# One layer of a hybrid decoder on one core: values transposed straight from their projection, and S5's output products tied to the next step

## The chip, the cores and the metric

The kernel runs on one core of one Trainium2 chip. The metric is the device time of one execution in microseconds, the median over several. PE is TensorE, DVE is VectorE, ACT is ScalarE, POOL is GpSimd, and SP is SyncE, which issues loads. Each engine works through its own queue in order and waits on semaphores that other engines and DMAs raise.

## The reference

One layer, 1024 tokens of width 1024. A normalised input `h` is projected once; two token mixers read the projection, S5 (a diagonal complex state space model) and DSA (attention over the 256 keys that an indexer scores highest); both are gated, merged and projected out.

```python
def hybrid_layer(x, c, ...):
    shift, scale, gate = jnp.split(jax.nn.silu(c) @ w_mod + b_mod, 3, axis=-1)
    h = rms_norm(x, norm_g) * (1 + scale) + shift
    xa, za, q, k, v, zb, qi, ki, wi, ga, gb = jnp.split(h @ w_in, IN_SPLITS, axis=-1)
    ya = jax.nn.gelu(s5_mixer(xa, a_re, a_im, b_re, b_im, c_re, c_im, d_skip, log_dt))
    g = ya @ w_glu + b_glu
    ya = ((g[..., :512] * jax.nn.sigmoid(g[..., 512:])) * jax.nn.silu(za)) @ w_a_o
    yb = dsa_mixer(q, k, v, qi, ki, wi)          # 8 query heads, one key and value head of 64
    yb = (yb * jax.nn.silu(zb)) @ w_b_o
    merged = jax.nn.sigmoid(ga) * ya + jax.nn.sigmoid(gb) * yb
    return x + gate * (merged @ w_out)
# s5_mixer: h_t = A h_(t-1) + B u_t per group of 16 channels (64 complex states), y_t = Re(C h_t) + D u_t
# dsa_mixer: score = sum over index heads of w * relu(qi . ki); keep the top 256 causal keys; softmax(q . k) v
```

## The kernel before, in words

All large products keep fp32 accuracy by splitting each operand in a high and a low half and multiplying three times, high by high, high by low and low by high (`three`, lines 137 to 139). A weight tile arrives as `*_w` from SP's queue, ACT casts the high half `*_wh`, DVE subtracts for the low half `*_wl` (`split`, lines 77 and 78). `project` makes one 128-row slice of the projection in two pieces of 512 tokens, 24 of these dense matmuls each, 48 a slice.

The input is transposed and normalised first, then xa, qi and ki are projected and the indexer's scores made, up to about 183 us. From there three things run beside each other until about 450 us:

- The **dense projections** on PE: q1 to q3, kv (keys in rows 0 to 63, values in rows 64 to 127), ga0 to ga7, gb0, gb1, zb0 to zb3. Their results leave through ACT (`gates`, lines 706 to 714) into a staging buffer of 128x1024 fp32, of which the pool `stage` has three, and are spilled to memory.
- The **S5 loop** (lines 584 to 683): eight steps q of four groups each. POOL prepares `mt` and `en` (lines 601 to 611). PE transposes `mt` (L614), and makes the kernel `k` (L621). ACT copies k, POOL adds the skip term (L630), and eight small DMAs from ACT's queue lay it out as the block matrix `mk` (L633). PE makes the states' input `s` (L637), ACT copies it out as `sp` (L643), DVE rotates, scans and rotates back (lines 655 to 672) and leaves the states `hs` (four subtractions and additions, the last of L672). PE then makes y from `mk` and the input (L676) and from `en` and `hs` (L678), four pairs into one bank, and ACT applies gelu and stores `yd`. `hs` has one buffer, `en` and `mk` have two.
- The **search** for the 256th score on DVE: twelve bisection steps of counts over the scores (`count`, L770), then the exact choice (lines 815 to 821). It ends in a flag `rows_ok` by which all engines branch; a slower path is taken only when the flag says so.

The order of instructions on each engine is made by the framework's scheduler, which follows data dependences, `order(later, earlier)` (an ordering without a wait) and `pace`, which ties dense matmuls behind given leads. Pools of buffers give further waits.

The values' way before: ACT copies rows 64 to 127 of kv into the staged tile `vraw` (`with_v`, L700), which is stored to memory as `vd` (L704). After the gate products (L737) a staged tile `vt` is loaded from `vd` (L751), once a staging buffer is free; PE transposes it in eight pieces into `v_ps` (L754), ACT and DVE split it into the halves of `v_s` (L77, L78). Then PE adds up the flag (L829), DVE casts it to `rows_ok` (L831), loads it to a register and branches (L833), and attention starts with the logits `l` (L894) and DVE's `S` (L897), with the dense matmuls of gb2 beside them.

Of the kernel before, what the change touches and what calls it, by code (L numbers as in the profile page):

```python
# [9 lines left out]
F32 = mybir.dt.float32  # L10
F32R = mybir.dt.float32r
BF = mybir.dt.bfloat16
I32 = mybir.dt.int32
AF = mybir.ActivationFunctionType
# [6 lines left out]
L = 1024  # L21
NT = L // 128
# [12 lines left out]
def tile_hybrid(ctx, tc, x, c, norm_g, w_mod, b_mod, w_in, a_re, a_im, b_re, b_im,  # L35
                c_re, c_im, d_skip, log_dt, w_glu, b_glu, w_a_o, w_b_o, w_out,
                final_g, out):
    nc = tc.nc
# [15 lines left out]
    spill = ctx.enter_context(tc.tile_pool(name="spill", bufs=1, space=DRAM))  # L54

    def bank(name):
        return ps1.tile([128, 512], F32, name=name, tag="b1")
# [10 lines left out]
    ident = const.tile([128, 128], F32, name="ident")  # L68
# [4 lines left out]
    def staged(name, dtype=F32, shape=(128, L)):  # L73
        return stage.tile(list(shape), dtype, name=name, tag="sg")

    def split(src, hi, lo, hi_eng=None, lo_eng=None):
        (hi_eng or nc.scalar.copy)(hi, src)  # L77
        (lo_eng or nc.vector).tensor_sub(lo, src, f32(hi))  # L78

    def order(later, earlier):  # L80

        tc.add_manual_dep(later.ins, earlier.ins.name, mybir.DependencyInfo(
            mybir.DependencyClass.NoSync, mybir.DependencyReason.DATA), reason="order")
# [78 lines left out]
    yds = []  # L162
    qd = spill.tile([8, 128, L], F32, name="qd")
    kd = spill.tile([2, 128, L], F32, name="kd")
    vd = spill.tile([64, L], F32, name="vd")
    zad = spill.tile([4, 128, L], F32, name="zad")
    zbd = spill.tile([4, 128, L], F32, name="zbd")
    gad = spill.tile([ND, 128, L], F32, name="gad")
# [3 lines left out]
    p2 = s5.enter_context(tc.tile_pool(name="p2a", bufs=1))  # L172
# [168 lines left out]
    with ExitStack() as st:  # L341
# [117 lines left out]
        ps = bank("wi_ps")  # L459
# [121 lines left out]
    mks = [p2.tile([128, 4, T, 16], F32, name=f"mk{e}") for e in range(2)]  # L581
    for mk in mks:
        nc.gpsimd.memset(mk, 0.0)
    for m in range(4):
        u_sb = p2.tile([128, 8, 128], F32, name=f"u{m}", tag="u", bufs=2)
        nc.scalar.dma_start(u_sb, uds[m].rearrange("g p s c -> (p s) g c"))
        yd = spill.tile([T, 16, 8, 128], F32, name=f"yd{m}")
        for half in range(2):
# [45 lines left out]

            ps = bank(f"s{q}_ps")
            for g in range(4):
                nc.tensor.matmul(ps[:, 128 * g:128 * g + 128], mi[:, g], us[:, g],  # L637
                                 start=True, stop=True)
            sp = p2.tile([128, 2, 2, 128], F32, name=f"sp{q}", tag="sp", bufs=2)
            pv = ps.rearrange("p (j e c) -> p e j c", j=2, e=2)  # L640
            for e in range(2):
# [27 lines left out]
            for e in range(2):  # L669
                a = slice(64 * e, 64 * e + 64)  # L670
                nc.vector.tensor_sub(hs[0:64, e:4:2, 1:], ra[a, 0, :, 0:127], rb[a, 1, :, 0:127])
                nc.vector.tensor_add(hs[64:128, e:4:2, 1:], ra[a, 1, :, 0:127], rb[a, 0, :, 0:127])  # L672
            ps = bank(f"y{q}_ps")
            for g in range(4):
                o = ps[:, 128 * g:128 * g + 128]
                nc.tensor.matmul(o, mk[:, g].rearrange("p t q -> p (t q)"), us[:, g],  # L676
                                 start=True, stop=False)
                nc.tensor.matmul(o, en[:, g, 1:9].rearrange("p t q -> p (t q)"), hs[:, g],  # L678
                                 start=False, stop=True)
            yg = p2.tile([128, 4, 128], F32, name=f"yg{q}", tag="yg", bufs=1)  # L680
            nc.scalar.activation(yg.rearrange("p g c -> p (g c)"), ps, AF.Gelu_apprx_tanh)
            nc.scalar.dma_start(yd[:, :, 4 * half:4 * half + 4].rearrange("t p g c -> (t p) g c"), yg)
        yds.append(yd)


    pace([], 0)
# [14 lines left out]
            yield ps, sl  # L701

    stack_k(with_v(project(w_in, K, 128, h_hi, h_lo, ND, "kv")), kd[0], kd[1], "k")
    nc.scalar.dma_start(vd, t[64:128])  # L704

    def gates(c0, ms, dst, silu, name):

# [38 lines left out]
    nc.sync.dma_start(f32(att_k), kd.rearrange("e p n -> p e n"))  # L746
    att_q = staged("qt0", F32R, (128, 8, 128))
    nc.sync.dma_start(f32(att_q), qd[:, :, 0:128].rearrange("h p n -> p h n"))
    att_v = kpool.tile([128, NT, 128], F32R, name="v_s")
    vt = staged("vt")  # L750
    nc.sync.dma_start(vt[0:64], vd)  # L751
    ps = bank("v_ps")
    for j in range(NT):
        nc.tensor.transpose(ps[:, 64 * j:64 * j + 64], vt[0:64, 128 * j:128 * j + 128], ident[:64, :64])  # L754
    split(ps.rearrange("p (j d) -> p j d", j=NT), att_v[:, :, 0:64], att_v[:, :, 64:128])


    for i in range(2):
# [351 lines left out]
```

## Time and profile before

| what | value |
|---|---|
| median of 3 runs | 911.64 us (910.56 to 913.61) |
| profiled execution, own time | 913.2 us |
| its span, first to last instruction | 911.4 us |
| mean granted clock of TensorE | 0.975 |
| instructions | 12005 |
| busy: DVE, ACT, POOL | 655.6 us (72%), 406.5 us (45%), 138.2 us (15%) |

The profile is of one execution. It lists busy time by engine, waits by line with the event that ended them, and the clock that TensorE was granted, as a share of 2.4 GHz. A wait at the head of an engine's queue holds up everything behind it on that engine. Idle time of an engine matters only where another engine, or the end, waits for it.

### The profile page before, as it was taken

To read this page: it belongs to the slowest core of one execution; us is meant where nothing else is said; L and a number is where in the kernel's file an instruction comes from. 1 tells how busy PE (TensorE), PEld (TensorE's weight loads), DVE (VectorE), ACT (ScalarE), POOL (GpSimd) and SP (SyncE) were. 2 spreads that over 40 slices of the span, in tenths; PEclk is the share of its full clock that TensorE was granted. 3 is DMA by queue.
4 is the path that set the end of the run, shared out by engine and by line. 5 is a ranking of instruction groups with operands and counts; after the bars stand their busy time and mean duration, and the time that the engine had idled before them with its cause. 6 is when DMAs were issued, how large, how long until landed. Compare 5 with 4: busy or idle time off the path is not lost.

```text
span 911.4 us, 12005 instructions
## 1 busy us (share of the span) xinstructions
PE 853.0 (94%) x4105; PEld 703.9 (77%) x4105; DVE 655.6 (72%) x1381; ACT 406.5 (45%) x803; POOL 138.2 (15%) x244
## 2 busy tenths in 40 slices
PE   4999999989889998999769999999999999999996
PEld 4887788877668877888558888887888888777885
DVE  5665898498989894687226677668987786956753
ACT  7553576354355542332225564457555443432311
POOL 0000100079446943000000000000000000221000
PEclk9799999999999998999969999999999999999999
DMA  9925611463443332573423323135314323644331
GB/s 328 315 65 131 147 49 47 74 181 89 121 117 119 110 111 65 183 263 92 116 70 97 92 83 112 47 105 151 103 47 129 92 81 93 198 150 149 139 131 54
DMA packets 124388, 110.38 MB, mean 121 GB/s; under 512 B 20954, under 2 KB 108066, under 8 KB 124324
## 3 DMA queue, kind: packets, MB, share of 16 engines
q1 hardware_dynamic: 96386, 77.46, 28.3%
q10 hardware_dynamic: 27938, 32.13, 12.0%
q8 instruction: 32, 0.52, 0.2%
q14 instruction: 32, 0.26, 0.1%
HBM read 76.67 MB, written 26.48 MB: 113 GB/s over the span
## 4 chain that ended last, share of the span: by engine, by line
PE 52%; DVE 13%; issue 4%; DMA 4%; ACT 2%; ACTq 2%; POOL 0%; DVEq 0%; SPq 0%
PE l L894 4%; DVE cj L770 3%; PE gb_ps L137 3%; PE gb_ps L138 3%; PE gb_ps L139 3%; PE pt L919 3%; PE o_ps L139 3%; PE o_ps L138 3%; PE o_ps L137 3%; PE pv L939 2%; PE pv L938 2%; PE ao_ps L139 2%; PE ao_ps L137 2%; PE ao_ps L138 2%; PE zb_ps L138 2%
## 5 line engine op out<-in xcount | busy, mean ns | idle before, releaser
L78 POOL TENSOR_TENSOR wo_l<-wo,wo_h 128x1024 fp32r<-128x1024 f32 x5 | 12.2, 2447 | 459.0 <-ACT wo_h L77 429.8
L770 DVE TENSOR_SCALAR_CACHE_REDUCE cj<-score,mid 128x1024 bf16<-128x1024 f32 (+2 forms) x72 | 67.6, 939 | 14.2 <-ACT mid L793 8.8
L897 DVE CUSTOM_DVE_ANT_0 S<-l,bias 128x384 f32<-128x384 f32 (+5 forms) x96 | 52.6, 553 | 26.5 <-PE l L894 23.4
L908 ACT ACTIVATE S<-S,stt 128x128 f32<-128x128 f32 (+7 forms) x64 | 49.1, 770 | 40.1 <-DVE stt L905 39.9
L77 ACT CAST ph<-pt 128x512 fp32r<-128x512 f32 x72 | 41.3, 584 | 43.4 <-PE pt L919 38.4
L78 DVE TENSOR_TENSOR pl<-pt,ph 128x512 fp32r<-128x512 f32 x72 | 48.8, 686 | 9.1 <-ACT ph L77 8.7
L894 PE MATMUL l<-k_s,qt 128*128 128x384 f32 (+5 forms) x192 | 50.2, 349 | 4.9 <-issue 4.9
L138 PE MATMUL gb_ps<-h_lo,gb_wh 128*128 128x512 f32 x128 | 51.4, 402 | 0.0
L137 PE MATMUL gb_ps<-h_hi,gb_wh 128*128 128x512 f32 x128 | 51.4, 401 | 0.0
L138 PE MATMUL o_ps<-wo_l,m_hi 128*128 128x512 f32 (+1 forms) x136 | 51.3, 378 | 0.0
L139 PE MATMUL o_ps<-wo_h,m_lo 128*128 128x512 f32 (+1 forms) x136 | 51.0, 377 | 0.1
L139 PE MATMUL gb_ps<-h_hi,gb_wl 128*128 128x512 f32 x128 | 51.1, 399 | 0.0
L139 PE MATMUL ga_ps<-h_hi,ga_wl 128*128 128x512 f32 x128 | 50.9, 397 | 0.0
L137 PE MATMUL ga_ps<-h_hi,ga_wh 128*128 128x512 f32 x128 | 50.7, 396 | 0.0
L138 PE MATMUL ga_ps<-h_lo,ga_wh 128*128 128x512 f32 x128 | 50.3, 393 | 0.0
L475 ACT ACTIVATE r<-s 128x512 f32<-128x512 f32 (+3 forms) x80 | 39.7, 525 | 23.2 <-PE s L471 15.4
L137 PE MATMUL o_ps<-wo_h,m_hi 128*128 128x512 f32 (+1 forms) x136 | 49.4, 377 | 0.2 <-ACT wo_h L77 0.2
L480 DVE SCALAR_TENSOR_TENSOR score<-r,wi_t,score 128x512 f32<-128x512 f32 (+3 forms) x70 | 42.1, 652 | 7.5 <-ACT r L475 6.6
L919 PE MATMUL pt<-ident,S 128*128 128x128 f32 x288 | 46.1, 272 | 0.0
L919 PEld LDWEIGHTS pt<-ident,S 128*128 128x128 f32 x288 | 36.5, 140 | 10.4
L471 PE MATMUL s<-ki_s,qi_s 128*128 128x384 f32 (+3 forms) x160 | 42.1, 355 | 1.8 <-DVE wi_t L464 1.3
L894 PEld LDWEIGHTS l<-k_s,qt 128*128 128x128 f32 x192 | 34.4, 191 | 10.4 <-issue 5.0
(402 smaller groups left out, 2400.7 us busy)
## 6 DMA issues: line engine op xcount, KB each, us to landing
wm<-in_w_mod_dram SPq DMA_DIRECT2D x16, 512.0 KB, 6.5
x_sb<-in_x_dram SPq DMA_DIRECT2D x8, 512.0 KB, 5.4
ga_w<-in_w_in_dram SPq DMA_DIRECT2D x8, 512.0 KB, 4.0
gad<-gas ACTq DMA_DIRECT2D x8, 512.0 KB, 2.6
gb_w<-in_w_in_dram SPq DMA_DIRECT2D x8, 512.0 KB, 4.4
wg<-in_w_mod_dram SPq DMA_DIRECT2D x8, 512.0 KB, 4.8
gbd<-gbs ACTq DMA_DIRECT2D x8, 512.0 KB, 3.1
qt<-qd SPq DMA_DIRECT2D x8, 512.0 KB, 4.0
```

The lines of the kernel that those rows point to most:

```text
L77: (hi_eng or nc.scalar.copy)(hi, src)
L78: (lo_eng or nc.vector).tensor_sub(lo, src, f32(hi))
L137: paced(nc.tensor.matmul(ps, wh, rh, start=first, stop=False))
L138: paced(nc.tensor.matmul(ps, wh, rl, start=False, stop=False))
L139: mm = nc.tensor.matmul(ps, wl, rh, start=False, stop=last)
L471: mm = nc.tensor.matmul(ps[:, :n], qs[:, h, 128 * i:128 * i + 128], ks[:, e, o:o + n], start=e == 0, stop=e == 1)
L480: nc.vector.scalar_tensor_tensor(dst, r[:, :n], wi_t[:, i, h:h + 1], dst, op0=OP.mult, op1=OP.add)
L770: nc.vector.tensor_scalar(j, src, at, None, op0=op, op1=OP.add, accum_out=dst)
L894: mm = nc.tensor.matmul(ps[:, :n], qt[:, 4 * e2 + 2 * j + g], ks[:, e, o:o + n], start=e == 0, stop=e == 1)
L897: nc.vector.tensor_tensor_reduce(out=S[:, o:o + n], in0=ps[:, :n], in1=bias[i][:, o:o + n], scale=1.0, scalar=NEG, op0=OP.add, op1=OP.max, ...
L908: nc.scalar.activation(S2[j], S2[j], AF.Exp, scale=0.125, bias=nm[:, j:j + 1], accum_out=sm[:, j:j + 1])
L919: mm = nc.tensor.transpose(ps[:, 128 * j:128 * j + 128], Ss[i, g, j][:, 128 * kb:128 * kb + 128], ident)
```

## The change

`vd`, `vt` and their two DMAs are gone: the transposes read rows 64 to 127 of the staged `vraw` tile, with the matching corner of the identity, and stand in the program right behind the keys' spill. The y products, their gelu and their store move to a function `outputs`, which is called in the following step behind the s products; its first matmul is ordered behind the last s product. The last call stands behind the loop.

```diff
@@ -162,7 +162,6 @@
     yds = []
     qd = spill.tile([8, 128, L], F32, name="qd")
     kd = spill.tile([2, 128, L], F32, name="kd")
-    vd = spill.tile([64, L], F32, name="vd")
     zad = spill.tile([4, 128, L], F32, name="zad")
     zbd = spill.tile([4, 128, L], F32, name="zbd")
     gad = spill.tile([ND, 128, L], F32, name="gad")
@@ -581,6 +580,23 @@
     mks = [p2.tile([128, 4, T, 16], F32, name=f"mk{e}") for e in range(2)]
     for mk in mks:
         nc.gpsimd.memset(mk, 0.0)
+    ready = []
+
+    def outputs(q, half, mk, us, en, hs, yd, behind_):
+
+        ps = bank(f"y{q}_ps")
+        for g in range(4):
+            o = ps[:, 128 * g:128 * g + 128]
+            mm = nc.tensor.matmul(o, mk[:, g].rearrange("p t q -> p (t q)"), us[:, g],
+                                  start=True, stop=False)
+            if g == 0:
+                order(mm, behind_)
+            nc.tensor.matmul(o, en[:, g, 1:9].rearrange("p t q -> p (t q)"), hs[:, g],
+                             start=False, stop=True)
+        yg = p2.tile([128, 4, 128], F32, name=f"yg{q}", tag="yg", bufs=1)
+        nc.scalar.activation(yg.rearrange("p g c -> p (g c)"), ps, AF.Gelu_apprx_tanh)
+        nc.scalar.dma_start(yd[:, :, 4 * half:4 * half + 4].rearrange("t p g c -> (t p) g c"), yg)
+
     for m in range(4):
         u_sb = p2.tile([128, 8, 128], F32, name=f"u{m}", tag="u", bufs=2)
         nc.scalar.dma_start(u_sb, uds[m].rearrange("g p s c -> (p s) g c"))
@@ -634,8 +650,10 @@
 
             ps = bank(f"s{q}_ps")
             for g in range(4):
-                nc.tensor.matmul(ps[:, 128 * g:128 * g + 128], mi[:, g], us[:, g],
-                                 start=True, stop=True)
+                last_s = nc.tensor.matmul(ps[:, 128 * g:128 * g + 128], mi[:, g], us[:, g],
+                                          start=True, stop=True)
+            if ready:
+                outputs(*ready.pop(), last_s)
             sp = p2.tile([128, 2, 2, 128], F32, name=f"sp{q}", tag="sp", bufs=2)
             pv = ps.rearrange("p (j e c) -> p e j c", j=2, e=2)
             for e in range(2):
@@ -670,17 +688,9 @@
                 a = slice(64 * e, 64 * e + 64)
                 nc.vector.tensor_sub(hs[0:64, e:4:2, 1:], ra[a, 0, :, 0:127], rb[a, 1, :, 0:127])
                 nc.vector.tensor_add(hs[64:128, e:4:2, 1:], ra[a, 1, :, 0:127], rb[a, 0, :, 0:127])
-            ps = bank(f"y{q}_ps")
-            for g in range(4):
-                o = ps[:, 128 * g:128 * g + 128]
-                nc.tensor.matmul(o, mk[:, g].rearrange("p t q -> p (t q)"), us[:, g],
-                                 start=True, stop=False)
-                nc.tensor.matmul(o, en[:, g, 1:9].rearrange("p t q -> p (t q)"), hs[:, g],
-                                 start=False, stop=True)
-            yg = p2.tile([128, 4, 128], F32, name=f"yg{q}", tag="yg", bufs=1)
-            nc.scalar.activation(yg.rearrange("p g c -> p (g c)"), ps, AF.Gelu_apprx_tanh)
-            nc.scalar.dma_start(yd[:, :, 4 * half:4 * half + 4].rearrange("t p g c -> (t p) g c"), yg)
+            ready.append((q, half, mk, us, en, hs, yd))
         yds.append(yd)
+    outputs(*ready.pop(), last_s)
 
 
     pace([], 0)
@@ -701,7 +711,12 @@
             yield ps, sl
 
     stack_k(with_v(project(w_in, K, 128, h_hi, h_lo, ND, "kv")), kd[0], kd[1], "k")
-    nc.scalar.dma_start(vd, t[64:128])
+
+    att_v = kpool.tile([128, NT, 128], F32R, name="v_s")
+    ps = bank("v_ps")
+    for j in range(NT):
+        nc.tensor.transpose(ps[:, 64 * j:64 * j + 64], t[64:128, 128 * j:128 * j + 128], ident[64:128, 64:128])
+    split(ps.rearrange("p (j d) -> p j d", j=NT), att_v[:, :, 0:64], att_v[:, :, 64:128])
 
     def gates(c0, ms, dst, silu, name):
 
@@ -746,13 +761,6 @@
     nc.sync.dma_start(f32(att_k), kd.rearrange("e p n -> p e n"))
     att_q = staged("qt0", F32R, (128, 8, 128))
     nc.sync.dma_start(f32(att_q), qd[:, :, 0:128].rearrange("h p n -> p h n"))
-    att_v = kpool.tile([128, NT, 128], F32R, name="v_s")
-    vt = staged("vt")
-    nc.sync.dma_start(vt[0:64], vd)
-    ps = bank("v_ps")
-    for j in range(NT):
-        nc.tensor.transpose(ps[:, 64 * j:64 * j + 64], vt[0:64, 128 * j:128 * j + 128], ident[:64, :64])
-    split(ps.rearrange("p (j d) -> p j d", j=NT), att_v[:, :, 0:64], att_v[:, :, 64:128])
 
 
     for i in range(2):
```

On PE the order around y5 moves so (a letter and number name a tile and the step q; hs5 are step 5's states, ga4 and ga5 dense projections). Before, 22 dense matmuls lie between the last y4 product and the first y5 product that reads hs5; these rows follow them:

```order
L139 MATMUL ga5_ps_3350<-h_hi3_249,ga5_wl_3321 128x512
L678 MATMUL y5_ps_2501<-hs5_2495,en5_2438 128x128
L676 MATMUL y5_ps_2501<-u2_2290,mk1_1901 128x128
L678 MATMUL y5_ps_2501<-hs5_2495,en5_2438 128x128
L676 MATMUL y5_ps_2501<-u2_2290,mk1_1901 128x128
L678 MATMUL y5_ps_2501<-hs5_2495,en5_2438 128x128
L676 MATMUL y5_ps_2501<-u2_2290,mk1_1901 128x128
L678 MATMUL y5_ps_2501<-hs5_2495,en5_2438 128x128
L621 MATMUL k6_ps_2534<-en6_2521,bx_1809 16x128 x4
L637 MATMUL s6_ps_2552<-u3_2513,mi6_2532 128x128 x4
L137 MATMUL ga5_ps_3350<-h_hi4_250,ga5_wh_3320 128x512
```

Now 32 dense matmuls lie between the last y4 product and these rows:

```order
L139 MATMUL ga5_ps_3360<-h_hi6_251,ga5_wl_3331 128x512
L637 MATMUL k6_ps_2521<-en6_2508,bx_1808 16x128 x4
L653 MATMUL s6_ps_2539<-u3_2500,mi6_2519 128x128 x4
L590 MATMUL y5_ps_2544<-u2_2277,mk1_1900 128x128
L594 MATMUL y5_ps_2544<-hs5_2494,en5_2425 128x128
L590 MATMUL y5_ps_2544<-u2_2277,mk1_1900 128x128
L594 MATMUL y5_ps_2544<-hs5_2494,en5_2425 128x128
L590 MATMUL y5_ps_2544<-u2_2277,mk1_1900 128x128
L594 MATMUL y5_ps_2544<-hs5_2494,en5_2425 128x128
L590 MATMUL y5_ps_2544<-u2_2277,mk1_1900 128x128
L594 MATMUL y5_ps_2544<-hs5_2494,en5_2425 128x128
L630 MATMUL mt7_ps_2594<-ident_75,mt7_2583 128x128 x4
```

y5's products moved from ahead of k6 and s6 to behind them, all eight together, and come 10 dense matmuls later. Counted in dense matmuls from the start of the program, the last products of y0 to y7 stand behind 655, 687, 756, 815, 926, 948, 998 and 1085 before, and behind 690, 722, 756, 821, 925, 957, 1011 and 1052 now. The first transposes of mt1 move from behind 588 to straight behind s0, at 531. POOL's instructions mu2, mt2, eu2 and mt3, which stood at the end of the rotation tables' products (lines 571 to 576) and behind it, stand among them now.

On PE the passage into attention, before:

```order
L139 MATMUL zb3_ps_3864<-h_hi7_253,zb3_wl_3834 128x512
L737 MATMUL gate0_3894<-gsum_3497,ones_80 1x512
L737 MATMUL gate1_3897<-gsum_3497,ones_80 1x512
L754 MATMUL v_ps_3915<-ident_75,vt_3913 128x64 x8
L829 MATMUL flag_ps_4358<-ones_80,sound_4354 1x1
L833 UNCONDITIONAL_BRANCH
L894 MATMUL l0_0_0_0_0_4958<-k_s_3908,qt0_3910 128x128 x2
L894 MATMUL l0_0_0_1_0_4963<-k_s_3908,qt0_3910 128x128 x2
```

and now:

```order
L139 MATMUL zb3_ps_3874<-h_hi7_252,zb3_wl_3844 128x512
L752 MATMUL gate0_3904<-gsum_3507,ones_80 1x512
L752 MATMUL gate1_3907<-gsum_3507,ones_80 1x512
L837 MATMUL flag_ps_4354<-ones_80,sound_4350 1x1
L902 MATMUL l0_0_0_0_0_4954<-k_s_3918,qt0_3920 128x128
L841 UNCONDITIONAL_BRANCH
L902 MATMUL l0_0_0_0_0_4954<-k_s_3918,qt0_3920 128x128
L902 MATMUL l0_0_0_1_0_4959<-k_s_3918,qt0_3920 128x128 x2
```

The transposes of V are gone from between the gate and the flag (they stand behind y7 now), and the first product of the logits stands ahead of PE's branch. On DVE the order gate sum, `rows_ok`, register load, branch is the same in both; the subtraction for `v_s`, which stood behind the branch, stands 1030 dense matmuls into the program. In the new order the four logits products are followed by 14 dense matmuls of gb2, and these by a logits product that needs a bank which DVE frees behind its branch.

## Rows read from the trace of the kernel before

**Rows 1.** Part 1 of the page: busy time, share of the span, instructions.
```profile
PE 853.0 (94%) x4105; PEld 703.9 (77%) x4105; DVE 655.6 (72%) x1381; ACT 406.5 (45%) x803; POOL 138.2 (15%) x244
```

**Rows 2.** PE's waits from 180 to 480 us: in total, times, longest.
```profile
PE v_ps L754 <- DMA vt<-vd: 10.4, 1, 10.4
PE y_ps L678 <- DVE hs L672: 9.0, 7, 2.4
PE y_ps L676 <- DMA mk<-k: 5.4, 2, 3.6
PE l L894 <- issue: 4.9, 1, 4.9
```

**Rows 3.** Windows: length, PE, PEld, DVE, ACT, POOL busy (x), PEclk, DMA, GB/s.
```profile
300.00:342.00 42.00, 39.12 (x195) 31.72 (x193) 37.87 (x64) 22.05 (x60) 29.17 (x52) 1.00 0.36 107
365.00:449.00 84.00, 84.00 (x383) 68.46 (x380) 55.08 (x91) 24.49 (x37) 0.31 (x1) 1.00 0.51 165
449.00:466.00 17.00, 1.72 (x13) 1.13 (x11) 3.46 (x6) 2.94 (x4) 0.00 (x0) 0.62 0.28 78
```

**Rows 4.** Timeline, 444 to 468 us: start, length, engine, line, [idle before <-releaser].
```profile
444.63 0.37 SPq L748 DMA_DIRECT2D qt<-qd  x1
...
448.41 1.02 PE L737 MATMUL gate<-gsum,ones 128*1 128x512 f32 x2
...
450.95 0.67 DVE L738 TENSOR_TENSOR bgate<-bgate,gate 1x512 f32<-1x512 f32 x1
...
456.17 0.52 SPq L751 DMA_DIRECT2D vt<-vd  x1
...
459.80 1.08 PE L754 MATMUL v_ps<-ident,vt 64*128 64x64 f32 x8 [10.37 <-DMA vt<-vd]
...
461.04 0.15 DVE L831 CAST rows_ok<-flag_ps 1x1 int32<-1x1 f32 x1 [9.42 <-PE flag_ps L829]
...
465.12 0.69 DVE L78 TENSOR_TENSOR v_s<-v_ps,v_s 128x512 fp32r<-128x512 f32 x1 [3.93 <-DVEq L833]
...
465.91 1.09 PE L894 MATMUL l<-k_s,qt 128*128 128x128 f32 x4 [4.91 <-issue]
...
466.61 0.29 DVE L897 CUSTOM_DVE_ANT_0 S<-l,bias 128x128 f32<-128x128 f32 x1 [0.80 <-PE l L894]
```

**Rows 5.** Chain of waits before 480 us: start, length, what.
```profile
451.05 5.07 DMA zbd<-zbs
```

**Rows 6.** Windows of PE alone: length, PE busy (x), granted clock, DMA, GB/s.
```profile
345.00:352.00 7.00, 6.78 (x31) 0.59 0.10 37
466.00:470.50 4.50, 4.50 (x14) 0.54 0.96 271
```

**Rows 7.** Timeline of PE, 326 to 352 us.
```profile
333.41 0.49 PE L678 MATMUL y_ps<-hs,en 128*128 128x128 f32 x2 [1.46 <-DVE hs L672]
...
342.70 0.46 PE L678 MATMUL y_ps<-hs,en 128*128 128x128 f32 x2 [1.56 <-DVE hs L672]
...
345.23 0.80 PE L678 MATMUL y_ps<-hs,en 128*128 128x128 f32 x2 [1.84 <-DVE hs L672]
...
350.97 0.47 PE L137 MATMUL ga_ps<-h_hi,ga_wh 128*128 128x512 f32 x1
```

**Rows 8.** Timeline of DVE and of POOL, four stretches of 222 to 370 us.
```profile
224.84 6.51 DVE L78 TENSOR_TENSOR kv_wl<-kv_w,kv_wh 128x1024 fp32r<-128x1024 f32 x1
...
342.24 1.44 POOL L611 TENSOR_TENSOR en<-en,eu 128x512 f32<-128x512 f32 x1
...
343.98 1.20 DVE L672 TENSOR_TENSOR hs<-ha,hb 64x254 f32<-64x254 f32 x1
352.79 0.69 DVE L655 TENSOR_TENSOR ra<-sp,ct 128x512 f32<-128x512 f32 x1 [7.62 <-ACT sp L643]
...
359.94 0.42 DVE L672 TENSOR_TENSOR hs<-ha,hb 64x254 f32<-64x254 f32 x1
369.19 1.23 DVE L78 TENSOR_TENSOR gb_wl<-gb_w,gb_wh 128x1024 fp32r<-128x1024 f32 x1 [8.83 <-ACT gb_wh L77]
```

## The prediction, on record before the run

> **What bounds the kernel now.** I read the page's busy shares first: TensorE (PE) works 94% of the span [rows 1], so a saving must come out of the 58 µs in which PE stands, or of stretches at the lower of its two clocks, 1.2 instead of 2.4 GHz. The table of PE's waits from 180 to 480 µs says where it stands near the change [rows 2]: 10.4 µs once for `vt<-vd`, 4.9 µs once as "issue" before the logits, 9.0 µs in seven waits of S5's y products for `hs`, and 5.4 µs in two waits for the `mk` DMAs. The windows split this into two stages [rows 3]. From 449 to 466 µs PE is busy 1.72 of 17 µs: the passage into attention, where nothing else runs either. Before it, 365 to 449 is busy for 84.00 of 84 µs: nothing is to be had there. From 300 to 342 PE is busy 39.12 µs and DVE 37.87 of 42: the S5 stage, where two engines are both nearly full, and PE's small holes are the DVE's lateness.
>
> The timeline of the passage [rows 4] is then read as a chain. PE's gate products end at 449.43 (448.41 + 1.02). The chain of waits gives 5.07 µs to the spill of `zbs` [rows 5], whose landing frees a staging buffer for `vt`; its load is issued at 456.17, and the transposes start at 459.80 and end at 460.88. Flag, `rows_ok` and DVE's branch follow. DVE picks up the low half of `v_s` at 465.12, 3.93 µs after `rows_ok` ended at 461.19; that subtraction ends at 465.81, and the first logits start at 465.91 and end at 467.00. So the 4.9 µs of "issue" are, as I read it, a wait for DVE, which is held up by its branch.
>
> **The change, V.** The round trip through memory goes: a 256 KB store and load, the buffer that they needed, and with them the wait of 10.4 µs. Eight transposes and two halves of the split remain, moved to a place in the middle of the projections, behind y7; DVE's half there takes 0.69 [rows 4], after its last `hs`. The `vraw` tile now holds one of three staging buffers until then, so the `ga` tiles share two; each is filled in 48 dense matmuls, 10.6 µs at 0.22 [rows 3], which leaves time to spill it, and the first `wg` loads wait on the queue SP until the transposes: they feed a sum that is needed at the gate only, some 80 µs later. I cost this at nothing; without that cover a late `wg` would stop SP's weight loads behind it. PE now goes gate, flag, first logits product, branch, and the rest. What is late next is `rows_ok`, which stands on DVE behind the second gate sum: that ends at 451.62 (450.95 + 0.67) [rows 4], so `rows_ok` ends at 451.77 and the logits run from about 451.9 to 453.0, if `qt0` is there: it is issued at 444.63, and the load of `vt`, half as large, took 3.63 µs from its issue to the transposes; twice that would be 451.9, so it is not late. They ended at 467.00, so **14.0 µs** go. DVE still needs 3.93 µs for its branch, until 455.7, but 14 dense matmuls stand on PE before a product that needs a buffer which DVE frees after the branch; at 84.00 µs for 383 matmuls, 0.22 each [rows 3], they take 3.1 µs, to 456.1, and DVE's first S, 0.29 µs, is done at 456.0. The branch is just covered. I also take back half-clock time: the granted clock is 0.54 from 466.0 to 470.5 [rows 6], which loses 4.5 × 0.46 = 2.1 µs. PE would now stand 2.4 µs (449.43 to 451.9), where it stood 16; whether that still lowers the clock the rows don't say, and I count 1.5 of the 2.1 as regained. The transposes cost at most their 1.08 µs in their new place, at half clock there as here; about half. V's part is −14.0 − 1.5 + 0.5 = **−15.0 µs**. Bounds: with the branch uncovered, only the wait for `vt` goes, less one for what is late next, −9.5; with all of the half clock back and the transposes free, −16.1.
>
> **The change, y.** The same 64 products run, none is added. They are tied behind the next step's s products, so PE asks for `hs` later. This pays only where PE was early; DVE decides when `hs` exists. Two points pin the result. First, y4: its last products stand behind 925 dense matmuls in the change and behind 926 now, and DVE has the same instructions ahead of `hs4`. PE waited there 1.46 µs [rows 7] and will wait again, because earlier waits that shrink (the two for `mk`, y1's two for `hs`) merely let PE arrive sooner at the same `hs4`. So nothing before 334 µs counts, also not the new waits there, such as the transposes of `mt1`, now straight behind s0. Second, y5: now 22 dense matmuls lie between y4 and y5, and PE waits 1.56 and 1.84 µs [rows 7] for `hs5`, which DVE ends at 345.18 [rows 8]; from then on the granted clock is low, 0.59 over the 7 µs from 345 [rows 6]. In the change 32 dense matmuls and the k6 and s6 products come first. PE leaves y4 about 2 µs after its 333.41, at 335.5, is through the 32 at 342.5 (0.22 each), and waits for `en6`, which GpSimd ends at 343.68 [rows 8]. From 345.23 to 350.97 [rows 7] PE did y5's last five products, k6 and s6 in 5.74 µs; at full clock that is some 3.0, and three y products more make 3.7. So k6, s6 and y5 end at 347.4, past `hs5`, with 957 dense matmuls behind them. Now that point, with 948 behind it, is 350.97, and nine more make it 353.0. That is **−5.6 µs**, with no wait left here that is longer than the 1.2 µs for `en6`. After this PE has no wait to the end of S5, now as then. Bounds: if `en6` or `hs5` come later by what the two old waits were, 0 is left, and 3 µs worse if the clock falls twice; if `hs4` itself comes sooner, since some of the 5.3 µs that `kv_wl` lost (6.51 against 1.23 of its kind [rows 8]) returns, and y4's wait of 1.46 with it, −5.6 − 5.3 − 1.5 = −12.4.
>
> **Sum.** −15.0 − 5.6 = −20.6 from the profiled execution's 913.2 µs, which gives 892.6. That execution lay 1.6 above the median of 911.64, so the forecast is **891 µs**. A measurement of this kernel tells 0.3%, some 2.7 µs.
>
> **A rule that speaks against it.** The rows of DVE and GpSimd [rows 8] show `kv_wl`, a subtraction of two operands in SBUF, taking 6.51 µs, beside the 1.23 of the `gb_wl` of the same shape when GpSimd was idle; the `hs` subtractions took 1.20 beside GpSimd's `en` and 0.42 alone. The Trainium skill, "SBUF — State Buffer", section "Who interferes with whom", states that a VectorE instruction with two SBUF inputs contends with a GpSimd instruction that reads SBUF, and that the loser is blocked for the whole instruction; the trace agrees in kind. In the change GpSimd is given mu2, mt2 and mt3 earlier, inside the rotation's row of products, so one more such block may fall ahead of `hs4`. Its price from the rows is 6.51 − 1.23 = 5.3 µs, by which `hs4`, and all behind it, would come later: 891 + 5.3 = **896**.
>
> **Rivals.**
> (a) *The branch stays bare.* The logits, or the product that ends the 14 matmuls, wait for DVE as now. For: "issue" is 4.9 µs and is not a wait for V [rows 2]. Against: the order puts a logits product in front of PE's branch, and DVE's subtraction of V is gone. V gives −9.5: 911.64 − 9.5 − 5.6 = 896.5.
> (b) *S5's waits only change names.* y5 then waits behind `en6` or `hs5` as long as now. For: both engines are nearly full [rows 3]. Only V counts: 897.
> (c) *DVE gets ahead.* With fewer blocks `hs4` is early, and S5 gives −12.4: 884.
> (d) *The block by the port*, above: 896.
> (e) *Slower.* `hs` has one buffer: `hs(q+1)` can't be written before y(q) has read `hs(q)`, and y(q) now stands behind s(q+1) in PE's order. If PE reaches each y late and DVE, in order, stands at the next `hs` with the search queued behind it, the two engines take turns. One step's DVE work from its first product to the end of `hs` is 7.6 µs undisturbed (352.79 to 360.36) [rows 8]; with 2 µs of k and s products beside it eight steps expose 8 × 5.6 = 45 µs, in place of 14.4 of waits [rows 2] and the 2.9 of half clock at 345 (7 × 0.41, [rows 6]), while V still gives 15: 911.64 − 15 − 17.3 + 45 = 924. It decides from 32.3/8, 4.0 µs a step. Against: between s(q+1) and the end of y(q) the order has 0 to 140 dense matmuls, and none for y1, y2 and y5 alone, so the others would have to be late as well.
>
> **How the numbers follow.** Forecast 0.50; (a) 0.12; (b) 0.17; (c) 0.09; (d) 0.07; (e) 0.05. The range runs from 884, case (c), to 902, where V gives 9.5 and S5 nothing (911.64 − 9.5). All but (e) are faster by over 0.3%; a mild form of (e) would be within it. So faster 0.93, same 0.03, slower 0.04.
>
> **What would show it.** Right: no `vt` row; under 3 µs between gate and logits; the first S some 4 µs after `rows_ok`, with gb products beside it; a wait of 1 to 2 µs at y4; under 1 µs at y5, and a clock near 1 from 345 on. Wrong: a PE wait of over 4 µs at the logits or the first gb products (a); y5 waiting over 3 µs (b); `hs4` before 331 (c) or after 338 (d); DVE idle behind y (e).

## The result and the profile after

| | before | changed |
|---|---|---|
| median (19 runs each, one chip) | 913.57 us (909.23 to 916.88) | 907.51 us (904.63 to 911.04) |
| profiled execution, own time | 913.2 us | 910.25 us |
| its span | 911.4 us | 908.5 us |
| mean granted clock | 0.975 | 0.979 |

The ratio is 0.9937, with a 95% interval of 0.9923 to 0.995: faster by 0.6%, some 6 us, where about 20 were forecast; outside the range.

Part 1 of the page of the changed kernel (busy time, share, instructions) already shows something that the change did not add: DVE runs the same 1381 instructions as in [rows 1], and is busy 12.8 us longer.

```profile
PE 854.2 (94%) x4105; PEld 704.4 (78%) x4105; DVE 668.4 (74%) x1381; ACT 407.1 (45%) x803; POOL 138.0 (15%) x244
```

PE's waits from 160 to 480 us (total, times, longest) say that the waits were traded. The wait for `vt` [rows 2] is gone and the "issue" is 2.3 instead of 4.9. But y4 waits 5.7 at once for `hs`, kv waits 7.3 for DVE, and gb1 and a logits product have waits of over 2 us.

```profile
PE y_ps L594 <- DVE hs L690: 9.4, 4, 5.7
PE kv_ps L137 <- DVE q_tl L78: 7.3, 1, 7.3
PE gb_ps L137 <- ACT gbs L726: 2.4, 1, 2.4
PE l L902 <- issue: 2.3, 1, 2.3
PE l L902 <- DVE stt L905: 2.3, 1, 2.3
```

**S5.** The windows of the changed kernel (length, then PE, PEld, DVE, ACT, POOL busy, clock, DMA, GB/s) answer to [rows 3]. From 300 to 342 PE works 36.13 us where it was 39.12, and DVE 40.16 where it was 37.87, the time of a blocked instruction being counted as busy: DVE became the bound of this stage.

```profile
449.00:466.00 17.00, 12.93 (x56) 9.05 (x54) 3.76 (x6) 4.48 (x5) 0.00 (x0) 1.00 0.52 153
...
300.00:342.00 42.00, 36.13 (x177) 29.42 (x175) 40.16 (x59) 18.52 (x53) 28.46 (x57) 0.98 0.28 81
```

DVE's timeline (start, length, what) has the two rows that fill it. The subtraction for `kv_wl`, 6.51 in [rows 8], takes 10.05, and that for ga5 takes 10.45, where the same row of the kernel before took 4.46. Neither instruction has changed.

```profile
227.36 10.05 DVE L78 TENSOR_TENSOR kv_wl<-kv_w,kv_wh 128x1024 fp32r<-128x1024 f32 x1
...
322.18 10.45 DVE L78 TENSOR_TENSOR ga_wl<-ga_w,ga_wh 128x1024 fp32r<-128x1024 f32 x1
332.55 0.87 DVE L778 TENSOR_SCALAR_CACHE_REDUCE cj<-score,mid 128x640 bf16<-128x640 f32 x1
```

POOL's timeline from 227 to 237 us is what stands beside the first: products of the rotation without a gap. The last ends at 236.32, `kv_wl` at 237.41.

```profile
227.43 1.06 POOL L617 TENSOR_TENSOR mt<-prr,bx 128x512 f32<-128x512 f32 x1
...
233.85 1.25 POOL L574 TENSOR_TENSOR ct<-ct,rt 128x512 f32<-128x512 f32 x1
235.07 1.25 POOL L575 TENSOR_TENSOR sn_t<-sn_t,rv 128x512 f32<-128x512 f32 x1
```

Before, the same row had a hole: POOL's next instruction, the addition to `k`, waited 2.66 us for ACT's copy. `kv_wl` ran in it and ended at 231.35.

```profile
229.20 1.06 POOL L602 TENSOR_TENSOR mu<-pir,by 128x512 f32<-128x512 f32 x1
232.92 0.31 POOL L630 TENSOR_TENSOR k<-k,dg 16x64 f32<-16x64 f32 x1 [2.66 <-ACT k L625]
```

For ga5 no hole was closed. POOL's row comes later in the change: its rotation products of 128x512 start at 321.19 instead of 316.41, and an `mt` more stands at the end. The subtraction met the row with 9.4 us of it left. Before, it met 3.4, and got in ahead of POOL's `dg`, which took 1.27 us instead of its usual 0.28. The last product of the row in the changed kernel, then the kernel before:

```profile
330.49 1.06 POOL L617 TENSOR_TENSOR mt<-prr,bx 128x512 f32<-128x512 f32 x1
```
```profile
322.12 4.46 DVE L78 TENSOR_TENSOR ga_wl<-ga_w,ga_wh 128x1024 fp32r<-128x1024 f32 x1
...
325.46 1.27 POOL L627 TENSOR_TENSOR dg<-dsk,ident 16x64 f32<-16x64 f32 x1
```

So `kv_wl` ended 6.1 us later than before. `hs0` ended 9.5 later (256.56 against 247.02), `hs3` 5.5, and after ga5's block `hs4` 7.7 (341.98 against 334.24). PE's row at y4, against 1.46 of wait at 333.41 in [rows 7]:

```profile
341.16 0.80 PE L594 MATMUL y_ps<-hs,en 128*128 128x128 f32 x2 [5.68 <-DVE hs L690]
```

y4's products ended at 344.3 instead of 335.5, 8.8 us late. Step 5 then did what was forecast of it. k6, s6 and y5 ran at 353.10 without a wait, and y5 ended at 357.0. Before, as many dense matmuls (957) lay behind PE at 353.0, by the count of the prediction. So 8.8 had become 4.0: step 5 gave 4.8.

**gb1.** At 405 PE waits for a staging buffer, and the window of 405 to 415 us (length, PE busy, clock, DMA, GB/s) is at part clock. Before, PE was busy for 49.00 of the 49 us from 400 on, at 1.00.

```profile
405.44 0.79 PE L137 MATMUL gb_ps<-h_hi,gb_wh 128*128 128x512 f32 x1 [2.35 <-ACT gbs L726]
```
```profile
405.00:415.00 10.00, 9.56 (x35) 0.83 0.24 87
```

ACT's rows there name who held the buffer, `gsum`, the sum over `wg` on DVE, whose inputs lie in the same three staging buffers. Ahead of it on ACT stands a copy of the search, `bias`, which waited 5.08 for DVE, in whose queue the additions to `gsum` lie as well. In the kernel before, ACT waited for `gsum` too, but PE did not yet stand behind ACT: it asked at 398.50, 0.7 us after ACT's first copy, so that chain was just in time. The changed kernel, and then the one before:

```profile
403.59 0.84 ACT L829 ACTIVATE bias<-cj_h 128x768 bf16<-128x768 bf16 x1 [5.08 <-DVE cj_h L828]
404.79 1.08 ACT L726 ACTIVATE gbs<-gb_ps 128x512 f32<-128x512 f32 x2 [0.35 <-DVE gsum L740]
```
```profile
397.19 1.09 ACT L711 ACTIVATE gbs<-gb_ps 128x512 f32<-128x512 f32 x2 [3.10 <-DVE gsum L725]
```

PE came to this point 4.6 us later than before (403.09 against 398.50), the sum 7.4 later (its last row starts at 405.33, at 397.94 before). The first `wg` load was issued at 378.92, and at 370.92 before; the profile puts its wait to the spill of a ga tile (4.8 us) and not to V's transposes, which start at 378.32. The gate products ended at 458.02, 8.6 us later than before.

**The passage** (timeline, 456 to 467 us):

```profile
456.14 1.88 PE L752 MATMUL gate<-gsum,ones 128*1 128x512 f32 x4
...
459.03 0.37 SPq L115 DMA_DIRECT2D gb_w<-in_w_in_dram  x1
...
459.64 0.33 ACTq L729 DMA_DIRECT2D zbd<-zbs  x1
460.13 0.14 DVE L839 CAST rows_ok<-flag_ps 1x1 int32<-1x1 f32 x1
...
460.37 0.63 PE L902 MATMUL l<-k_s,qt 128*128 128x128 f32 x4 [2.33 <-issue]
...
466.19 0.29 DVE L905 CUSTOM_DVE_ANT_0 S<-l,bias 128x128 f32<-128x128 f32 x1 [5.92 <-DVEq L841]
...
466.54 0.52 PE L902 MATMUL l<-k_s,qt 128*128 128x128 f32 x2 [2.29 <-DVE stt L905]
```

From the end of the gate to the first logits it takes 2.35 us, where it took 16.48 [rows 4]. DVE's branch takes 5.92 us and not 3.93; the 14 dense matmuls end before it does, and PE waits 2.29.

The account, in the profiled executions: +8.8 at y4, −4.8 in step 5, +4.6 up to the gate's end (2.35 of wait at gb1, 1.7 of part clock, the rest small), −14.1 to the logits, +2.3 behind them: −3.2. The spans differ by −2.9.

### The profile page after: what moved, and what is told of

Read it like the earlier page. It is cut to its first block, busy times and chain, and to the rows that moved or that the text cites. A ratio compares the mean times of both kernels' runs of the same rounds, so it can differ in the third digit from the quotient of the medians.

```text
span 908.5 us, 11989 instructions
## 1 busy us (share of the span) xinstructions
PE 854.2 (94%) x4105; PEld 704.4 (78%) x4105; DVE 668.4 (74%) x1381; ACT 407.1 (45%) x803; POOL 138.0 (15%) x244
```

## The experiments

The theory after the result: the values' part works, and the y part pays with longer blocks of two DVE subtractions by POOL's products, because it removes the pauses in which DVE got in. The rivals: the y part costs in itself, through PE's order; or the values' part costs through the staging buffer. All ratios are against the kernel before on the same chip.

**Each part alone.** v_only is the kernel before with the values' part of the diff; y_only the other part.

```diff
 # v_only                                # y_only
-vt round trip                           -y products at the end of step q
+transposes from vraw, behind kd         +outputs(q, ...) behind s(q+1)
 y products as before                    vt round trip as before
```

> Values transposed from the staged tile, y products as before. Theory (the loss of the change sits in S5: DVE's long subtractions kv_wl 10.05 us and ga5_wl 10.45 us beside GpSimd's row of products): here S5 is as before, kv_wl about 6.5 and ga5_wl about 4.5 us, hs4 ends near 334, and only the passage into attention shrinks, by about 11 us as in the trace of the change: 902 to 904 us. Rival (the staging buffer that vraw holds makes the gate's loads late, and that is the loss): 908 to 911 us, with a PE wait at gb1 of 2 us or more.

> y products one step later, values by way of memory as before. Theory: kv_wl and ga5_wl take about 10 us each as in the change, hs4 ends near 341, y5 gives back some 4.8 us, and the passage stays: 915 to 919 us, slower than before. Rival (S5 is slowed by the V part, not by the order of y): 905 to 909 us.

v_only: 904.62 us, ratio 0.992 (0.99 to 0.994). y_only: 919.15, ratio 1.0077 (1.0047 to 1.0107), slower. The whole change lies between them, but the parts do not add up: by the ratios v_only gains 7.3 us, y_only loses 7.0, and the whole gains 5.8. So on top of the values' part the y part costs 1.6 us, no more than the intervals leave open. A wait at gb1 is in all three, and so counts twice in the sum of the parts. PE's waits in y_only:

```profile
PE y_ps L595 <- DVE hs L691: 11.0, 4, 5.3
PE v_ps L765 <- DMA vt<-vd: 10.2, 1, 10.2
PE kv_ps L137 <- DVE q_tl L78: 7.3, 1, 7.3
```

Here `kv_wl` took 10.03 (6.54 in v_only) and `hs4` ended at 344.03 (335.48 in v_only). The y part alone brings the block, and costs. The wait at gb1 is in both, 2.6 in v_only and 2.4 in y_only, where no V lies in a staging buffer and the first `wg` is issued at 375.40. So the buffer that `vraw` holds is not needed for that wait. But it is enough for it: in v_only S5 is nearly as before, and yet a `wg` load waits 1.7 us for V's transposes, ACT copies gb1 at 399.85 instead of 397.19, and the gate ends at 453.13, 3.7 us later than before. The second rival explains a part of the loss, and not the y part's.

**Taking the subtractions off DVE.** lo_pool is the change with the low halves of kv and ga5 made on POOL, b_lo_pool the kernel before with the same.

```diff
-split(raw, hi, lo)
+split(raw, hi, lo, lo_eng=nc.gpsimd if name in ("kv", "ga5") else None)
```

> The change, with the low halves of the weights kv and ga5 subtracted by GpSimd, in its own queue, and not by DVE. Theory: DVE loses its two waits of 9 us each, hs4 ends at 334 or before, y4's wait for hs falls from 5.7 to under 2 us, the wait of kv for DVE's q_tl (7.3 us) goes: 897 to 901 us. Rival (the two subtractions only fill time that DVE would have spent waiting; the order of y makes hs late): 905 to 908 us, with DVE idle ahead of hs4.

> The kernel before, with the low halves of kv and ga5 subtracted by GpSimd. Theory: DVE gets back 5.3 us at kv and 3.2 us at ga5; PE's waits for hs (9.0 us in all) fall by about half: 907 to 911 us. Rival: the waits only move to GpSimd's en and mt, 913 us or more.

lo_pool: 896.17 us, ratio 0.9825 (0.9803 to 0.9847); the kv wait is gone and the `hs` waits are 3.7. But `hs4` came at 338.31 only. b_lo_pool: 913.51, ratio 1.001 (0.9991 to 1.0028), a miss: nothing gained. In both another DVE instruction stood in the row of products, one of 8 columns that takes 0.22 in the kernel before. lo_pool, DVE and the end of POOL's row:

```profile
323.67 7.17 DVE L825 TENSOR_SCALAR best<-ranks,cgt 128x8 f32<-128x8 f32 x1
```
```profile
328.27 1.28 POOL L574 TENSOR_TENSOR ct<-ct,rt 128x512 f32<-128x512 f32 x1
329.51 1.28 POOL L575 TENSOR_TENSOR sn_t<-sn_t,rv 128x512 f32<-128x512 f32 x1
```

and b_lo_pool, DVE:

```profile
325.05 5.92 DVE L817 TENSOR_SCALAR best<-ranks,cgt 128x8 f32<-128x8 f32 x1
```

The block belongs to the place and not to the instruction. Taking one instruction away passes it to the next that needs what POOL holds.

**Leaving products out.** rot_once builds the second rotation table no more.

```diff
-ct, sn_t = rotation(q)
+if q == 0: ct, sn_t = rotation(0)
```

> The change, with the second rotation table left out: steps 4 to 7 use the first table again, so their part of y is not the reference's, and GpSimd has some 21 us of products less around 305 to 330 us. Theory (DVE's two-operand instruction waits for the end of GpSimd's unbroken row): ga5_wl takes 1.2 to 2.5 us instead of 10.45, and hs4 ends at 334 or before. Rival (something else blocks DVE there, a DMA or its own queue): ga5_wl or the instruction behind it still takes over 6 us.

905.25 us in a single run. No low half of ga took more than 1.61 us and `hs4` ended at 323.53, 18 us sooner: without those products there is no block. Yet the time is only some 2 us below the change's median, and inside the range of the change's runs. Its waits were at y2 (4.12), y4 (2.98) and still 7.32 at kv. The first block was untouched, and the order was planned anew: 491 dense matmuls lie between y4 and the gate, where the change has 419, so PE asked for `hs4` that much sooner and waited for `hs` 8.3 us in all, against 9.4. That fits how little was left over; it was not tried apart.

**A pause on POOL.** The change, but POOL waits for `kv_wl` and `ga5_wl` ahead of the largest products of each table.

```diff
+after(rows_[0, 6], lows["kv"])
+after(rows_[8, 6], lows["ga5"])
```

> The change, with GpSimd made to wait, ahead of the largest products of each rotation table, until DVE has done kv_wl and ga5_wl: a gap in its row, no work moved. Theory: both subtractions take 1.2 to 2.5 us, hs4 ends at 335 or before, GpSimd loses 1 to 3 us a time: 896 to 901 us. Rival (as in the kernel before with the subtractions on GpSimd, the block falls on the next DVE instruction that needs it): another DVE instruction takes 5 us or more, 904 to 908 us.

895.26 us, ratio 0.9821 (0.9807 to 0.9834): by the ratios some 11 us less than the change. DVE's timeline and, below it, POOL's:

```profile
230.17 3.59 DVE L78 TENSOR_TENSOR kv_wl<-kv_w,kv_wh 128x1024 fp32r<-128x1024 f32 x1
...
319.07 5.61 DVE L78 TENSOR_TENSOR ga_wl<-ga_w,ga_wh 128x1024 fp32r<-128x1024 f32 x1
```
```profile
231.95 0.73 POOL L582 TENSOR_TENSOR sn_t<-sn_t,rv 128x256 f32<-128x256 f32 x1
233.91 1.04 POOL L578 TENSOR_TENSOR ct<-ct,wrot 128x512 f32<-128x512 f32 x1 [1.23 <-DVE kv_wl L78]
...
323.56 1.30 POOL L653 TENSOR_TENSOR k<-k,dg 16x64 f32<-16x64 f32 x1
```

POOL stood for 1.23 us, `kv_wl` took 3.59 instead of 10.05, and the wait at kv fell from 7.3 to 0.8. At ga5 POOL shows no wait: its products stand in another order there, the subtraction got in ahead of `k`, which took 1.30 instead of 0.31, and it took 5.61 instead of 10.45. No product is removed, and PE's order is nearly the change's: y0 to y3 stand at the same place among the dense matmuls, y4 to y7 behind 8 more. With POOL's rows opened the change is 1% faster than v_only; without that it was no faster than v_only. So the blocks are what the y part costs; how much each of the two openings gave was not tried.

**Freeing the staging buffer.** vearly is the change with `v_ps` in a bank of the dense pool, so that the planner puts the transposes behind 687 dense matmuls and not behind 1030, and `vraw` is freed sooner.

```diff
-ps = bank("v_ps")
+ps = psd.tile([128, 512], F32, name="v_ps", tag="d")
```

> The change, with v_ps in a bank of the dense projections instead of the small banks, which are handed out in program order behind S5's: the transposes come right behind kv, and the staging buffer of vraw is free some 110 us sooner. Theory (the buffer made the wg loads late): PE's wait of 2.4 us at gb1 for gbs and the slow clock behind it go: 902.5 to 905 us. Rival (wg is late because S5 is late, not because of the buffer): 906.5 to 909 us.

899.76 us, ratio 0.9869 (0.9852 to 0.9886), some 3 us below what was expected, and by the ratios 6 below the change. The wait at gb1 fell from 2.4 to 1.1, and the first `wg` was issued at 371.43. But the order changed with it: ga5's block is 7.67 long, and 24 more dense matmuls stand ahead of y4, whose wait fell to 1.69 although `hs4` ended at 342.89, later than in the change. PE is ahead of the change by some 4.5 us at y4 already (24 times 0.227, less 0.9), ahead of the `wg` loads, so most of the gain does not come by them.

**Together.** best1 is lo_pool with vearly, best2 is pause with vearly.

> The change with kv's and ga5's low halves on GpSimd, and v_ps in a dense bank. In the first without the second PE waited 6.2 us at gb1 for gbs, behind the wg loads. Theory: that wait goes with the slow clock behind it: 887 to 891 us. Rival (the wg loads stay late): 894 to 897 us.

> The change with the two pauses for GpSimd and with v_ps in a dense bank. The pauses gave 895.3, the bank took 7.7 us off the change. Theory (two separate causes, a block on DVE and late wg loads): the gains add up, 888 to 891 us, at least as good as the two low halves on GpSimd with the bank (892.5). Rival (one bound hides the other): 894 to 897 us.

best1: 892.46 us, ratio 0.9796 (0.9781 to 0.9812), over the 887 to 891 expected. In lo_pool, whose S5 is early, the third `wg` load is issued at 372.88 only, behind an addition to `gsum` that ended at 372.85, and gb1 waits 6.2; in best1 it is issued at 370.49, the wait is 1.6, and the time 3.7 us less, 2.6 by the ratios, whose intervals overlap. That fits a buffer held by `vraw`, but neither trace shows a load that waits for V's transposes. best2: **891.36 us** (888.67 to 892.63), ratio 0.9765 (0.9744 to 0.9785), the lowest median of all. PE's waits in best2, from 160 to 480 us:

```profile
PE y_ps L601 <- DVE hs L697: 3.6, 5, 1.3
PE l L911 <- issue: 2.3, 1, 2.3
PE ga_ps L143 <- DVE k_tl L78: 2.1, 1, 2.1
PE l L911 <- DVE stt L914: 2.0, 1, 2.0
...
PE kv_ps L143 <- DVE q_tl L78: 0.8, 1, 0.8
...
PE gb_ps L143 <- ACT gbs L733: 0.2, 1, 0.2
```

**The y part without the block.** v_best1 and v_best2 are best1 and best2 with the y products in their old place.

> As the version at 892.5 us (low halves of kv and ga5 on GpSimd, v_ps in a dense bank), but with y in its old place, in the same step. Theory (once DVE isn't blocked, asking for hs later pays at y4 and y5, where PE waited and the clock fell): 897 to 900 us, with waits for hs of 7 us or more in all. Rival (the delay of y is worth nothing by itself): 891 to 894 us.

> best2 with y in its old place: V moved early, GpSimd paused for the two subtractions, so that neither is blocked long in either kernel. The run v_best1 was meant to price the moved y products and had a DVE subtraction of 10.96 us in it that best1 has not, so it priced that as well. If moving y pays by itself (it gave about 5 us in y5's step of the change): DVE has no row over 6 us, and the ratio is 0.981 to 0.984, against best2's 0.9765. If y's place is worth nothing where DVE is not blocked: 0.975 to 0.978. If it is worth the 11 us of v_best1: 0.987 to 0.990 with no long row on DVE.

v_best1: 903.53 us, ratio 0.989 (0.9865 to 0.9914). v_best2: 906.06, ratio 0.9941 (0.9919 to 0.9964). Both are slower than expected, and neither prices the y part alone: in each the planner put another low half of ga into the row of products. v_best1 has one of 10.96 us at 307.74; v_best2, DVE and POOL:

```profile
311.28 9.79 DVE L78 TENSOR_TENSOR ga_wl<-ga_w,ga_wh 128x1024 fp32r<-128x1024 f32 x1 [2.48 <-ACT ga_wh L77]
```
```profile
317.69 1.30 POOL L609 TENSOR_TENSOR mt<-mt,mu 128x512 f32<-128x512 f32 x1
318.93 1.06 POOL L580 TENSOR_TENSOR sn_t<-ct,wrot 128x512 f32<-128x512 f32 x1
326.14 0.31 POOL L636 TENSOR_TENSOR k<-k,dg 16x64 f32<-16x64 f32 x1 [6.16 <-ACT k L631]
```

POOL's row ended at 319.99, the subtraction at 321.07. Of the 14.7 us between best2 and v_best2 (16 by the ratios) some 8.6 (9.79 less the 1.23 of an undisturbed one) may be this block. What the moved y products give with no block on either side stays open; the one clean figure is the 4.8 of step 5.

**The branch.** quiet is the change with the flag's product waiting until the last spill of `zbs` has landed, so that nothing is in flight when DVE branches.

```diff
+after(nc.tensor.matmul(flag, sound, ones, ...), spilled[-1])
```

> The change, with the flag's product made to wait for the landing of the last zbs spill, as the order of the kernel before did in effect: nothing but the branch is in flight then. A diagnosis, some 4 to 6 us slower than the change. Theory (DVE's branch is slow beside transfers: 5.9 us here with the gb weights and the spill in flight, 3.9 us before with none): from the end of rows_ok to DVE's next instruction 3.8 to 4.3 us. Rival (it hangs on the instructions and their place, not on transfers): 5.4 us or more.

912.30 us in a single run, the added wait being 6.7. DVE's timeline behind its branch:

```profile
463.67 0.14 DVE L846 CAST rows_ok<-flag_ps 1x1 int32<-1x1 f32 x1 [4.74 <-PE flag_ps L844]
467.85 0.29 DVE L912 CUSTOM_DVE_ANT_0 S<-l,bias 128x128 f32<-128x128 f32 x1 [4.03 <-DVEq L848]
```

4.03 us and not 5.92. Over all kernels: 3.93 (before, y_only), 4.14 (b_lo_pool) and 4.03 (quiet) where the branch follows the landing of the spill, and 5.51 to 5.92 in the others, which all have V moved; in the change the branch comes beside the load of `gb_w` and the spill. The same code branches, and quiet differs from the change in the wait alone. Which of the two transfers it is was not tried.

The traces show more of it. Between `rows_ok` and DVE's next instruction each of the fourteen has one packet of 8 KB on a DMA queue that the profile calls instruction (q14). It starts 2.0 to 2.2 us behind `rows_ok` in before, y_only, b_lo_pool and quiet, where the DMA engines are busy for 0.00 to 0.01 of the time, and 3.5 to 3.8 us behind it in the other ten (0.60 to 0.65 busy). From its start to DVE's next instruction it is 1.9 to 2.2 us in all of them. So the extra time passes before this packet starts; that DVE waits for this packet is not shown.

## Why the prediction was wrong

**The round trip of V, −14.0: right.** The gate's end to the first logits went from 16.48 us to 2.35, −14.1. `rows_ok` and then `qt0` were next in line, as worked out, and the logits stood in front of PE's branch.

**"The branch is just covered": wrong by 2.3 us.** The step took DVE's 3.93 from a row in which nothing was being transferred. In the change the branch runs earlier, beside a spill and a weight load, and takes 5.92. The 14 matmuls end at 464.25, 1.94 before the first S begins. With it went the regained clock of 1.5: the granted clock from 466 to 480 is 0.88, 0.85 before. The passage gave −14.1 + 2.3, about −12, instead of the −15.5 of its two terms there.

**"I cost this at nothing", the staging buffer: wrong, some 4 us came up to the gate, of which the buffer's share in the change is not separated.** The sentence let the 80 us until the gate cover the late `wg`. That is not where the cover ends: gb1's spill takes its buffer from the same three, 27 us behind the transposes, and ACT's wait for `gsum` in the kernel before, which I had not read, says that there was hardly any slack: PE asked 0.7 us after ACT's copy. It cost 2.35 of wait and 1.7 of clock. v_only has that wait with S5 nearly as before, and its gate ends 3.7 us late; y_only has it without `vraw`. Either is enough; in the change both may act.

**The y part, −5.6: its first pin failed, its second held.** The step that failed is "DVE has the same instructions ahead of `hs4`", from which I took `hs4` to stay at 334. It has the same instructions, and two of them took 9.5 us longer. So the moved y products did not only make PE ask later. By bringing POOL's `k` addition its input sooner, or moving it, they closed the hole in which `kv_wl` had got in, and they made POOL's second row some 5 us later, so that ga5's subtraction met 9.4 us of it instead of 3.4. y_only shows both without V's part (10.03 and 7.59 us; +7 us), and pause shows that opening POOL's rows undoes most of it. The second pin, step 5, was forecast at −5.6 and measured at −4.8.

Of the rivals, (d), the block by the port, was the mechanism, with "`hs4` after 338" as its sign: 341.98. It was given 0.07 and a single block of 5.3 us. There were two, and they cost 8.8 at y4. The mistake in its price was to take 6.51 − 1.23 for what a block costs. That row was itself a block that had ended early, at a pause of POOL; the price is the length of POOL's row that is left, 9 us here. The Trainium skill, "SBUF — State Buffer", section "Who interferes with whom", calls the loser blocked for the whole instruction of the other engine. The traces agree that it is blocked and not slowed, but a single POOL product took 1.0 to 1.3 us, and the blocked rows of 128x1024 took 3.6 to 11.0: here DVE waited for many products in turn. Elsewhere it waited for one: step 5's four rows of `hs` (64x254, 0.42 alone) took 1.19 to 1.40 us each beside POOL's products of 346 to 354 us. What decides between the two the rows do not show.

The sum by these steps: −14.1 + 2.3 for the passage, +4.6 up to the gate, +8.8 − 4.8 for y is −3.2 us in the profiled execution, where −20.6 was forecast. Of the 17.4 between, 9.6 lie in the y part (8.8 the blocks, 0.8 step 5), 4.1 on the way to the gate, and 3.7 in the passage (branch and clock). Cases (a), (b), (c) and (e) did not occur by their signs: the logits' waits are 2.3 each and not over 4, step 5 lost its waits, DVE did not get ahead, and the engines did not take turns.

## What to carry to other kernels

A moved step keeps another engine's instructions the same and still changes how long they take: where two engines compete for a port, look for the pauses of the one in which the other gets in, and ask whether the change closes them. A row that is already blocked gives the least price of a block, not its price; the price can be all the unbroken work left on the engine that holds the port, and an opening put there by hand can buy it back (some 11 us here for two). What two parts of a change cost apart need not add up: here both brought the wait at gb1, and the whole paid it once. A chain off the critical path is measured by the last engine that waits for it already, here ACT for `gsum`: where that engine waits, look for the slack there (0.7 us here), however far away the final consumer is.

## What the hardware showed that was not expected

- A DVE subtraction of 128x1024 with two SBUF operands that met POOL's rotation products waited for many of them in turn. It ended 1.09 us after the row's end for `kv_wl`, and 1.08 in v_best2, which leaves about its own 1.23 of work. A gap in POOL's row is not always needed: DVE got in ahead of `dg` (kernel before) and `k` (pause), which followed without one and took 1 us longer. Counts over the scores (one SBUF operand and a scalar per row) ran through the same rows at their usual 0.6 to 1.3 us. POOL's products were hardly longer for it, 1.03 to 1.32 us.
- A small instruction can be blocked as long: the 8-column `best` took 5.92 and 7.17 us in POOL's row, 1.84 in pause, where it met the end of one, and 0.22 to 0.23 where it met none. It reads one tensor and a scalar per row, as the counts do, so the number of operands alone doesn't tell which DVE instruction is blocked.
- From `rows_ok` over DVE's branch to its next instruction it took 3.93 to 4.14 us with no transfer under way, and 5.51 to 5.92 beside transfers. The Trainium skill, "Runtime: NRT & Kernel Launch", section "Instruction fetch mechanics", says that a taken branch out of the prefetched instructions has to wait for a DMA that fetches them. The runs agree in kind: the branch is slower where other DMAs run, and a packet of an instruction queue stands in each, at 2.0 to 2.2 us or at 3.5 to 3.8. That it is the fetch that DVE waits for is not shown.
